# A hybrid state-space and gated-recurrence block: another model for the instruction scheduler, and other steps for scan, GELU, carry and output weight loads

## The chip, the cores and the metric

The kernel runs on one core of one Trainium2 chip. The metric is the device time of one execution in microseconds; the time before is 1541.35 us, the median of 3 runs (1541.31 to 1543.61).

## What is computed

One decoder block over 2048 rows of width 1024, in float32. The input is normalised, projected once to 5632 columns, and split into two branches; their outputs are projected, gated, merged, projected again and added to the input.

```python
xn = rms_norm(h, norm_w)
u_a, z_a, q_b, f_b, i_b, og_b, z_b, g_a, g_b = jnp.split(xn @ w_in, SPLIT_POINTS, axis=-1)
# branch A: 32 groups, each a complex diagonal state of 64, by an associative scan over the rows
y = C h + d * u;  y = gelu(y);  y = y * sigmoid(y @ w_glu + b_glu);  y_a = y * silu(z_a)
# branch B: 4 heads, gated recurrence in chunks, output gate, norm per head
state = exp(last) * state + k exp(last - cum) v;  y_b = rms_norm(o * sigmoid(og)) * silu(z_b)
merged = sigmoid(g_a) * (y_a @ w_proj_a) + sigmoid(g_b) * (y_b @ w_proj_b)
out = rms_norm(h + merged @ w_out, final_norm_w)
```

## The kernel before, in words

The rows are worked in two halves of 1024 (a = 0 and 1). Every float32 operand of a large matmul is split into a rounded part and a rest (`split`, lines 118 to 120: one ACTIVATE on ScalarE for the first, one subtraction on VectorE for the second), and each product is three matmuls (high by high, high by rest, rest by high).

The stages follow each other. First some projections are done plainly (`plain`). Then comes a Strassen stage for the first half (`strassen(0, s0)`, 18 slices of 256 columns) and one for the second half (`strassen(1, s1)`, 22 slices). A slice is seven products of 12 matmuls of 512 columns (lines 458 to 460); its results gather in PSUM banks of a pool of four, are copied out on ScalarE (`snap`, L464) or added on VectorE (`total`, L467), and go to an `evac` function. Weights are split at their first use, stored to DRAM as `wc` and loaded from there in the second half (L375, three products ahead, in a ring of five buffers). Behind them stand, for each half, two GLU passes (`glu`), the merge of the branches (`merge`) and the output projection (`out_proj`), in which `narrow` does one half of the columns, one tile of 128 rows after the other.

Other work is laid beside these dense stages by hand. `timed(dense, n, events)` runs the dense generator for n steps and calls, before each step, the events that are due at it; `steps(ev, g, at)` puts the parts of a generator, divided by its `yield`s, at the steps of a list. So are laid out: the recurrence of branch B (`hgrn_block`, levels 0 to 8 and two more parts), the tables of the scan (`ssm_build`), the scan in 16 batches of four groups (`ssm_batch`: loads of WU and VM, for a = 0 the cosine and sine tables from E, matmuls into psg, the scan on VectorE, matmuls into psy, a store to y_d), `gelu` (a load of yy, four ACTIVATEs that reorder it, Square, two operations on VectorE, Sigmoid, a multiplication, a store to ya_d), `glu_prep` (reloads of that, and splits) and `out_w` (a load of the output weights, and splits).

TensorE's order is that of the program text (`tc.manual_schedule` for this engine). The order of ScalarE, VectorE, GpSimd and SyncE is made at build time by the framework's scheduler: it plays the program on a model of the chip and hands each engine, of the instructions that the model holds ready, the one that stands earliest in the text. On the chip each engine then runs its list in order. Nearly all loads and most stores are issued by SyncE (SP); some stores by ScalarE. Buffers come from pools with tags: `wr` (3 buffers, `wr4`), `wo` (5), `y` (2, `y4`), `s` (5), `e` (2), `r` (56).

## Time and profile before

| | before |
|---|---|
| median of 3 runs | 1541.35 us |
| the profiled execution | 1540.05 us |
| its span, first to last instruction | 1538.3 us |
| PE (matmul) busy | 1467.0 us, 95%, 7360 instructions |
| PEld (weight load) busy | 1207.3 us, 78% |
| DVE (VectorE) busy | 1100.8 us, 72%, 2409 instructions |
| ACT (ScalarE) busy | 637.6 us, 41%, 1391 instructions |
| DMA | 354.53 MB, mean 230 GB/s |

A matmul's busy time overlaps with that of its neighbours, so a busy PE is read together with the time from one start to the next. The granted clock is given as a share of 2.4 GHz. In a timeline row, the bracket at the end is the engine's idle time before the instruction and what ended it; the count after x is how many like instructions are merged in the row.

### The profile page before, as it was taken

Reading aid. Unit: us, or ns where it says so; the run is one execution under the profiler, and the core shown is the slowest. Engines: PE = TensorE matmul, PEld = TensorE weight load, DVE = VectorE, ACT = ScalarE, POOL = GpSimd, SP = SyncE. Lnnn points to the kernel's source line nnn. Section 1 sums busy time; section 2 is a strip of 40 time slices with the busy share of each in tenths; the row PEclk is TensorE's granted clock in tenths of the full one; section 3 lists DMA queues with packets and bytes.
Section 4 is the critical chain, followed back from the end, with each engine's and each line's share of the span. In section 5 each row is a group of like instructions: output and inputs, shape, how many; then the busy total and the mean of one; then the engine's idle time right before and its main releaser. Section 6 shows DMA issues by size and latency. Waiting matters only on the chain.

```text
span 1538.3 us, 21386 instructions
## 1 busy us (share of the span) xinstructions
PE 1467.0 (95%) x7360; PEld 1207.3 (78%) x7360; DVE 1100.8 (72%) x2409; ACT 637.6 (41%) x1391; POOL 3.6 (0%) x24
## 2 busy tenths in 40 slices
PE   7997999999999999999989999999989899899997
PEld 5776788788888777878878887788878688688886
DVE  5798688678678659956665887776649877765445
ACT  7456454454454634323323455333353332532222
POOL 0000000000000000000000000000000000000000
PEclk9998999999999999999999999999999999999999
DMA  9539778977977883786668559677977854854602
GB/s 336 175 115 305 284 278 295 316 255 269 331 264 286 285 271 119 186 245 197 231 201 313 174 163 294 217 259 264 327 236 234 266 184 137 274 171 131 212 14 103
DMA packets 192060, 354.53 MB, mean 230 GB/s; under 512 B 65680, under 2 KB 74896, under 8 KB 191952
## 3 DMA queue, kind: packets, MB, share of 16 engines
q1 hardware_dynamic: 163792, 328.00, 63.6%
q10 hardware_dynamic: 28160, 25.17, 4.8%
q8 instruction: 58, 0.95, 0.3%
q14 instruction: 50, 0.41, 0.1%
HBM read 214.17 MB, written 138.94 MB: 230 GB/s over the span
## 4 chain that ended last, share of the span: by engine, by line
PE 68%; DVE 15%; DMA 10%; ACT 3%; issue 3%; SPq 0%; ACTq 0%; DVEq 0%
PE pd L458 14%; PE pd L460 13%; PE pd L459 13%; PE pf L1284 3%; PE pf L1285 3%; PE pf L1286 3%; PE pp L1112 2%; PE pp L1111 2%; PE pp L1110 2%; PE sc L979 2%; DMA y_d<-T 1%; DVE w L120 1%; DMA xb<-in_xt_dram 1%; DMA xq<-xo_d 1%; PE pd L355 1%
## 5 line engine op out<-in xcount | busy, mean ns | idle before, releaser
L119 ACT ACTIVATE w<-rw 128x512 fp32r<-128x512 f32 x110 | 68.7, 628 | 112.7 <-PE pd L460 67.9
L1284 PE MATMUL pf<-ho,mh 128*128 128x512 f32 x256 | 101.2, 395 | 5.2 <-ACT mh L119 5.2
L1286 PE MATMUL pf<-ho,ml 128*128 128x512 f32 x256 | 100.6, 393 | 0.5 <-DVE ml L120 0.5
L1285 PE MATMUL pf<-lo,mh 128*128 128x512 f32 x256 | 100.3, 392 | 0.0
L464 ACT ACTIVATE u<-pd 128x512 f32<-128x512 f32 x80 | 47.5, 594 | 106.0 <-PE pd L460 103.3
L120 DVE TENSOR_TENSOR w<-rw,w 128x512 fp32r<-128x512 f32 x110 | 75.3, 685 | 16.9 <-ACT w L119 16.6
L467 DVE TENSOR_TENSOR u<-u,pd 128x512 f32<-128x512 f32 x80 | 54.8, 685 | 33.5 <-PE pd L460 22.8
L355 PE MATMUL pd<-xh,hw 128*128 128x512 f32 x128 | 52.4, 409 | 9.0 <-ACT hw L119 6.7
L1284 PEld LDWEIGHTS pf<-ho,mh 128*128 128x128 f32 x256 | 48.6, 190 | 15.4 <-ACT mh L119 5.5
L1286 PEld LDWEIGHTS pf<-ho,ml 128*128 128x128 f32 x256 | 48.4, 189 | 11.6 <-DVE ml L120 1.6
L1285 PEld LDWEIGHTS pf<-lo,mh 128*128 128x128 f32 x256 | 48.6, 190 | 9.9
L119 ACT ACTIVATE mh<-sgl 128x512 fp32r<-128x512 f32 x32 | 20.0, 629 | 86.7 <-DVE sgl L1227 86.3
L356 PE MATMUL pd<-xl,hw 128*128 128x512 f32 x128 | 51.2, 400 | 0.0
L357 PE MATMUL pd<-xh,lw 128*128 128x512 f32 x128 | 50.9, 397 | 0.0
L980 DVE COPY_PREDICATED s_buf<-masks,sc 128x256 f32<-128x256 uint8 x64 | 32.5, 508 | 25.0 <-PE sc L979 25.0
L1110 PE MATMUL pp<-yh,hpa 128*128 128x512 f32 x128 | 50.2, 392 | 0.0
L1112 PE MATMUL pp<-yh,lpa 128*128 128x512 f32 x128 | 49.9, 390 | 0.2 <-DVE lpa L120 0.2
L1111 PE MATMUL pp<-yl,hpa 128*128 128x512 f32 x128 | 50.0, 390 | 0.0
L1226 DVE TENSOR_TENSOR sgl<-sgl,pp 128x512 f32<-128x512 f32 x48 | 32.7, 683 | 23.0 <-PE pp L1112 22.9
L1016 DVE TENSOR_TENSOR Q<-Q,t 128x256 f32<-128x256 f32 x96 | 40.5, 422 | 10.0 <-PE sc L991 9.9
L974 ACT ACTIVATE KX<-K 128x128 f32<-128x128 f32 x128 | 32.6, 304 | 35.6 <-DVE K L1017 26.3
L979 PEld LDWEIGHTS sc<-Q,KX 128*128 128x128 f32 x256 | 38.0, 189 | 8.9 <-issue 1.8
(915 smaller groups left out, 4431.6 us busy)
## 6 DMA issues: line engine op xcount, KB each, us to landing
wc<-w SPq DMA_DIRECT2D x126, 512.0 KB, 3.4
w<-wc SPq DMA_DIRECT2D x126, 512.0 KB, 4.6
rw<-in_wi_dram SPq DMA_DIRECT2D x44, 512.0 KB, 4.6
sgl<-sg_d SPq DMA_DIRECT2D x48, 256.0 KB, 3.2
sg_d<-u ACTq DMA_DIRECT2D x32, 256.0 KB, 3.5
ro<-in_wo_dram SPq DMA_DIRECT2D x16, 512.0 KB, 5.1
hh<-in_xn_dram SPq DMA_DIRECT2D x32, 256.0 KB, 5.1
out_dram<-hh SPq DMA_DIRECT2D x32, 256.0 KB, 2.4
```

Of the source, the lines that this page charges most:

```text
L119: S.activation(hi, raw, AF.Copy)
L120: V.tensor_tensor(lo, raw, hi.bitcast(F32), op=ALU.subtract)
L458: mm(o, w[:, 0, k], xh, start=(first and k == 0), stop=False, skip_group_check=True)
L459: mm(o, w[:, 0, k], xl, start=False, stop=False, skip_group_check=True)
L460: mm(o, w[:, 1, k], xh, start=False, stop=(k == 3), skip_group_check=True)
L979: mm(ps[:, :, c, :], ch(kx, c), qp, start=True, stop=True)
L1110: mm(ps, hi[:, k, fs], yh, start=(k == 0), stop=False)
L1111: mm(ps, hi[:, k, fs], yl, start=False, stop=False)
L1112: mm(ps, lo[:, k, fs], yh, start=False, stop=(k == last))
L1284: mm(o, mh[:, ts_], hi, start=(kk == 0), stop=False)
L1285: mm(o, mh[:, ts_], lo, start=False, stop=False)
L1286: mm(o, ml[:, ts_], hi, start=False, stop=(kk == 7))
```

## The change

The tile context gets `schedule_with_timeline_sim=True`: the scheduler plays the program on another, the timeline model, before it orders the engines other than TensorE. Beside it the steps and the text order of several pieces are changed:

- `ssm_batch`: the loads are no longer all at the first part. For a = 0, E is loaded first, then after two parts W and U, then V and M; the stores of the cosine and sine tables stand behind the first use of psg. For a = 1 the tables, W and U come first, V and M a part later. The first part of a batch is at step -7 (was -5) for a = 0; in the second pass a batch is laid at 4 + 7i (was 6 + 7i).
- `gelu` is divided by `yield`s into five parts, which are put at steps of their own: the reordering copies three steps behind the load, the rest in the steps after.
- `hgrn_block`: the load of the carried state moves from the start of the block to level 6.
- `out_w` gets a `yield` between load and split, and its parts are put at other steps; `narrow` looks the split weights up when it uses them, not before it begins.
- `glu_prep(1, 0)` is one step later; the raw weights of the second half's first QF slice come from the pool `wr`, not `y`.

```diff
@@ -379,7 +379,7 @@
             wc_d[sl] = [dram.tile([128, 1024], F32, name=f"wc{sl}_{p}") for p in range(7)]
 
         def get(kh):
-            raw = (y4 if a and sl != SL_VO else wr4)(f"rw{n}_{kh}").rearrange("p (k n) -> p k n", k=4)
+            raw = (y4 if a and sl < SL_QF else wr4)(f"rw{n}_{kh}").rearrange("p (k n) -> p k n", k=4)
             nc.sync.dma_start(raw, wi[sl, kh])
             return raw[:, :, 0:128], raw[:, :, 128:256]
 
@@ -751,39 +751,39 @@
         sh = [128, 4, 8, 16]
         t4 = lambda n: sp.tile(sh, F32, name=f"{n}{a}{b}", tag="s")
         flat = lambda t: t.rearrange("p g a b -> p g (a b)")
-        WU = wu_pool(f"WU{a}{b}").rearrange("p (i g n) -> p i g n", i=2, g=4)
-        VM = vm_pool(f"VM{a}{b}").rearrange("p (i g n) -> p i g n", i=2, g=4)
-        Wt, U = WU[:, 0], WU[:, 1]
-        Vt, Mt = VM[:, 0], VM[:, 1]
-        nc.sync.dma_start(Wt, w_d[:, gs, :])
-        nc.sync.dma_start(U, u_d[a][b // 2][:, :, g0 : g0 + 4, :].rearrange("s p g c -> (s p) g c"))
-        nc.sync.dma_start(Vt, v_d[:, gs, :])
-        nc.sync.dma_start(Mt, m_d[:, gs, :])
-        CC, SS = t4("CC"), t4("SS")
         csv = lambda i: cs_d[b][:, i].rearrange("p (g a b) -> p g a b", g=4, a=8)
-        T = t4("T")
         if a == 0:
             E = sp.tile([128, 4, 48], F32, name=f"E{b}", tag="e", bufs=2)
             nc.sync.dma_start(E[:, :, 0:32], el_d[:, gs, :])
             nc.sync.dma_start(E[:, :, 32:48], eh_d[:, gs, :])
+            yield
+        CC, SS = t4("CC"), t4("SS")
+        T = t4("T")
+        if a == 0:
             lr_ = E[:, :, 0:16].unsqueeze(2).to_broadcast(sh)
             li_ = E[:, :, 16:32].unsqueeze(2).to_broadcast(sh)
             hr_ = E[:, :, 32:40].unsqueeze(3).to_broadcast(sh)
             hi_ = E[:, :, 40:48].unsqueeze(3).to_broadcast(sh)
-            yield
             V.tensor_tensor(CC, lr_, hr_, op=ALU.mult)
             V.tensor_tensor(T, li_, hi_, op=ALU.mult)
             yield
             V.tensor_tensor(CC, CC, T, op=ALU.subtract)
             V.tensor_tensor(SS, lr_, hi_, op=ALU.mult)
-            yield
-            V.tensor_tensor(T, li_, hr_, op=ALU.mult)
-            V.tensor_tensor(SS, SS, T, op=ALU.add)
-            nc.sync.dma_start(csv(0), CC)
-            nc.sync.dma_start(csv(1), SS)
         else:
             nc.sync.dma_start(CC, csv(0))
             nc.sync.dma_start(SS, csv(1))
+        WU = wu_pool(f"WU{a}{b}").rearrange("p (i g n) -> p i g n", i=2, g=4)
+        Wt, U = WU[:, 0], WU[:, 1]
+        nc.sync.dma_start(Wt, w_d[:, gs, :])
+        nc.sync.dma_start(U, u_d[a][b // 2][:, :, g0 : g0 + 4, :].rearrange("s p g c -> (s p) g c"))
+        yield
+        if a == 0:
+            V.tensor_tensor(T, li_, hr_, op=ALU.mult)
+            V.tensor_tensor(SS, SS, T, op=ALU.add)
+        VM = vm_pool(f"VM{a}{b}").rearrange("p (i g n) -> p i g n", i=2, g=4)
+        Vt, Mt = VM[:, 0], VM[:, 1]
+        nc.sync.dma_start(Vt, v_d[:, gs, :])
+        nc.sync.dma_start(Mt, m_d[:, gs, :])
         C2, S2 = flat(CC), flat(SS)
         yield
         ps = pss.tile([128, 4, 128], F32, name=f"psg{a}{b}", tag="pss")
@@ -793,6 +793,9 @@
         V.tensor_tensor(t1, ps, C2, op=ALU.mult)
         V.tensor_tensor(t2[0:64], ps[64:128], S2[64:128], op=ALU.mult)
         V.tensor_tensor(t2[64:128], ps[0:64], S2[0:64], op=ALU.mult)
+        if a == 0:
+            nc.sync.dma_start(csv(0), CC)
+            nc.sync.dma_start(csv(1), SS)
         yield
         V.tensor_tensor(t1, t1, t2, op=ALU.add)
         hv = h0[:, gs]
@@ -835,18 +838,22 @@
     GE = 2.0 * math.sqrt(2.0 / math.pi)
 
     def gelu(a, i):
-        ya = wr4(f"ya{a}{i}")
         yy = y4(f"yy{a}{i}").rearrange("p (t c) -> p t c", t=8)
         nc.sync.dma_start(yy, y_d[a][i].rearrange("t p g c -> (p g) t c"))
+        yield
+        ya = wr4(f"ya{a}{i}")
         for i4 in range(4):
             c0 = i4 * 256
             dst = ya[:, c0 : c0 + 256] if i4 % 2 == 0 else ya[:, c0 + 255 : (c0 - 1 if c0 else None) : -1]
             S.activation(dst.rearrange("p (c t) -> p t c", t=8), yy[:, :, i4 * 32 : i4 * 32 + 32], AF.Copy)
         q = yy.rearrange("p t c -> p (t c)")
         S.activation(q, ya, AF.Square)
+        yield
         V.tensor_scalar(q, q, 0.044715, 1.0, op0=ALU.mult, op1=ALU.add)
         V.tensor_tensor(q, q, ya, op=ALU.mult)
+        yield
         S.activation(q, q, AF.Sigmoid, scale=GE)
+        yield
         V.tensor_tensor(ya, ya, q, op=ALU.mult)
         nc.sync.dma_start(ft_d["ya", a, i], ya)
 
@@ -937,9 +944,6 @@
         K = h2("K" + n, "K")
         V.tensor_scalar(K, F, -1.0, 1.0, op0=ALU.mult, op1=ALU.add)
         Sb = s_buf[b]
-        if a == 1 and b == 0:
-            cin = e2("ci" + n)[:, 0:128]
-            nc.sync.dma_start(cin, carry_d[h])
         KX = h2("KX" + n, "x")
         V.tensor_tensor(KX, K, Q, op=ALU.mult)
         kh = hp.tile([128, 512], F32R, name="kh" + n, tag="st")
@@ -983,6 +987,9 @@
                     ps.rearrange("p a c (j m) -> p a (c j) m", m=m),
                 )
             elif lv <= 7:
+                if lv == 6 and a == 1 and b == 0:
+                    cin = e2("ci" + n)[:, 0:128]
+                    nc.sync.dma_start(cin, carry_d[h])
                 ps = psc.tile([128, 4, 128], F32, name=f"sc{n}_{lv}", tag="psc")
                 for hf in range(2):
                     for r in range(0, 128, 2 * m):
@@ -1252,6 +1259,7 @@
                 continue
             raw = wr4(f"ro{a}{nh}{kp}").rearrange("p (k n) -> p k n", k=2)
             nc.sync.dma_start(raw, wo[nh, kp])
+            yield
             res = ow[a, nh, kp] = []
             for k in range(2):
                 hi = pool.tile([128, 512], F32R, name=f"ho{a}{nh}{kp}{k}", tag="r")
@@ -1339,14 +1347,14 @@
                     if tt % 2:
                         yield
 
-        def narrow(nh, w):
+        def narrow(nh):
             for tt in range(8):
                 x_load(nh, tt)
                 if nh == 1:
                     V.tensor_scalar(fss[:, tt : tt + 1], fss[:, tt : tt + 1], -0.5 / D, -0.5 * EPS, op0=ALU.mult, op1=ALU.add)
                 o = psd.tile([128, 512], F32, name=f"pf{a}{nh}{tt}", tag="psd")
                 for kp in range(4):
-                    products(nh, kp, tt, o, w[kp])
+                    products(nh, kp, tt, o, ow[a, nh, kp])
                     if kp == 1:
                         yield
                 add_x(nh, tt, o)
@@ -1355,10 +1363,10 @@
                 yield
 
         if a == 0:
-            yield from narrow(0, [ow[a, 0, kp] for kp in range(4)])
+            yield from narrow(0)
         else:
             yield from wide(0, {})
-        yield from narrow(1, [ow[a, 1, kp] for kp in range(4)])
+        yield from narrow(1)
 
     def run(*gens):
         for g in gens:
@@ -1505,10 +1513,11 @@
         batches = [ssm_batch(0, b, wr4, wr4) for b in range(8)] + [ssm_batch(1, b, wr4, wr4) for b in range(2)]
         for i, g in enumerate(batches):
             t = 62 + 9 * i
-            for d in ((-5, -4, -3, -2) if i < 8 else (-3,)) + (0, 1, 2, 3, 6):
+            for d in ((-7, -4, -3, -2) if i < 8 else (-4, -2)) + (0, 1, 2, 3, 6):
                 ev.append((t + d, lambda g=g: step(g)))
             if i % 2:
-                ev.append(((101, 106, 118, 136, 151)[i // 2], lambda i=i: gelu(i // 8, i // 2 % 4)))
+                t = (98, 105, 116, 134, 150)[i // 2]
+                steps(ev, gelu(i // 8, i // 2 % 4), [t, t + 3, t + 4, t + 5, t + 6])
         steps(ev, glu_prep(0, 0), [146, 147, 148, 149])
         steps(ev, glu_w(), [150, 151, 152, 153])
         timed(d1, 154, ev)
@@ -1518,14 +1527,15 @@
         steps(ev, glu_prep(0, 1), [0, 1, 2, 3])
         for i in range(6):
             g = ssm_batch(1, i + 2, y4, wr4 if i < 2 else wo4f, (psm, "psm"))
-            t = 6 + i * 7
-            for d in (-3, 0, 1, 2, 3, 6):
+            t = 4 + i * 7
+            for d in (-4, -2, 0, 1, 2, 3, 6):
                 ev.append((t + d, lambda g=g: step(g)))
             if i % 2:
-                ev.append((t + 7, lambda i=i: gelu(1, i // 2 + 1)))
-        steps(ev, out_w(0, 0, range(4), rp), [14 + s for s in range(8)])
-        steps(ev, out_w(0, 1, range(4), rp), [28 + s for s in range(8)])
-        steps(ev, glu_prep(1, 0), [51, 52, 53, 54])
+                steps(ev, gelu(1, i // 2 + 1), [t + 7, t + 10, t + 11, t + 11, t + 12])
+        for kp in range(4):
+            steps(ev, out_w(0, 0, (kp,), rp), [12 + 2 * kp, 15 + 2 * kp, 16 + 2 * kp])
+            steps(ev, out_w(0, 1, (kp,), rp), ([24, 27, 28], [26, 29, 30], [36, 40, 40], [37, 41, 41])[kp])
+        steps(ev, glu_prep(1, 0), [52, 53, 54, 55])
 
         def lazy(f):
             yield from f()
@@ -1542,7 +1552,8 @@
         for i in range(8):
             steps(ev, yb_load(1, i // 2, i % 2), [i // 2 + 2, i // 2 + 4])
         steps(ev, out_w(1, 0, (0,), None), [21])
-        steps(ev, out_w(1, 1, (2, 3), rp), [26, 27, 28, 29])
+        for kp in (2, 3):
+            steps(ev, out_w(1, 1, (kp,), rp), [19 + 2 * kp, 22 + 2 * kp, 23 + 2 * kp])
         steps(ev, out_w(1, 1, (0, 1), None), [37, 38])
         mg1 = merge(1)
         ev += [(4, lambda: step(mg1)), (6, lambda: step(mg1))]
@@ -1636,7 +1647,7 @@
         args.append(nc.dram_tensor(f"in_{name}_dram", a.shape, mybir.dt.from_np(a.dtype), kind="ExternalInput").ap())
     o = nc.dram_tensor("out_0_dram", (L, D), F32, kind="ExternalOutput")
     args.append(o.ap())
-    with tile.TileContext(nc) as tc:
+    with tile.TileContext(nc, schedule_with_timeline_sim=True) as tc:
         hybrid_block(tc, *args)
     r = run_bass_kernel_spmd(nc, [arrays], core_ids=[0])
     return np.ascontiguousarray(_order(np.asarray(r.results[0]["out_0_dram"]).reshape(L, D))).reshape(1, L, D)
```

## Rows read from the trace of the kernel before

**Rows 1.** The page's line of busy time by engine, and the span with the mean granted clock.
```profile
PE 1467.0 (95%) x7360; PEld 1207.3 (78%) x7360; DVE 1100.8 (72%) x2409; ACT 637.6 (41%) x1391; POOL 3.6 (0%) x24
...
core 0: 1538.3 us, clock 0.984
```
**Rows 2.** The view of windows. Columns: the stretch in us, its length, then busy us (and instructions) of PE, PEld, DVE, ACT and POOL, the mean granted clock, the mean busy share of the 16 DMA engines, and GB/s.
```profile
120.00:160.00 40.00, 33.40 (x151) 27.62 (x150) 34.08 (x104) 23.36 (x55) 0.00 (x0) 0.89 0.93 321
...
240.00:280.00 40.00, 40.00 (x197) 33.63 (x196) 34.70 (x78) 18.67 (x41) 0.00 (x0) 1.00 0.82 297
...
500.00:560.00 60.00, 54.90 (x283) 43.58 (x282) 40.78 (x81) 36.31 (x85) 0.00 (x0) 0.97 0.81 274
...
760.00:800.00 40.00, 37.40 (x219) 31.01 (x218) 27.75 (x63) 11.70 (x28) 0.00 (x0) 1.00 0.67 205
800.00:840.00 40.00, 38.06 (x233) 31.26 (x232) 23.72 (x50) 9.79 (x24) 0.10 (x1) 0.96 0.90 315
...
1120.00:1145.00 25.00, 19.36 (x81) 15.63 (x80) 8.47 (x12) 9.70 (x16) 0.00 (x0) 0.86 0.68 227
...
1160.00:1200.00 40.00, 40.00 (x198) 33.66 (x197) 38.49 (x70) 11.55 (x19) 0.00 (x0) 1.00 0.72 241
1200.00:1240.00 40.00, 33.19 (x142) 26.57 (x141) 32.92 (x60) 15.57 (x28) 0.00 (x0) 0.87 0.84 280
...
1320.00:1360.00 40.00, 32.74 (x127) 25.67 (x126) 30.57 (x65) 20.94 (x38) 0.00 (x0) 0.91 0.73 246
```
**Rows 3.** The timeline of PE in a quiet stretch and behind a long wait.
```profile
269.75 0.39 PE L459 MATMUL pd<-X014l,w 128*128 128x512 f32 x1
...
271.34 0.39 PE L460 MATMUL pd<-X034h,w 128*128 128x512 f32 x1
...
1134.61 0.79 PE L458 MATMUL pd<-X105h,w 128*128 128x512 f32 x1 [5.64 <-ACT u L464]
...
1138.62 0.55 PE L458 MATMUL pd<-X135h,w 128*128 128x512 f32 x1
```
**Rows 4.** The timeline of ACT at the end of the second Strassen stage.
```profile
1130.90 2.09 ACT L844 ACTIVATE ya<-yy 128x256 f32<-128x256 f32 x4 [6.73 <-DMA yy<-y_d]
...
1133.98 0.58 ACT L464 ACTIVATE u<-pd 128x512 f32<-128x512 f32 x1
```
**Rows 5.** The timelines of ACT, DVE and PE where the merge of the first half ends and its output projection begins.
```profile
1211.94 2.14 ACT L844 ACTIVATE ya<-yy 128x256 f32<-128x256 f32 x4 [3.57 <-DMA yy<-y_d]
...
1215.21 0.69 DVE L847 TENSOR_SCALAR yy<-yy 128x1024 f32<-128x1024 f32 x1 [3.41 <-ACT yy L846]
...
1223.83 0.66 DVE L1227 TENSOR_TENSOR sgl<-sgl,sgl 128x512 f32<-128x512 f32 x1
...
1225.21 0.79 PE L1284 MATMUL pf<-ho,mh 128*128 128x512 f32 x1 [5.22 <-ACT mh L119]
```
**Rows 6.** The timelines of ACT, SP and PE around the first GLU pass of the second half.
```profile
1300.02 0.58 ACT L831 ACTIVATE T<-psy 128x512 f32<-128x512 f32 x1
...
1316.09 0.33 SPq L851 DMA_DIRECT2D ya_d<-ya  x1
...
1322.70 0.52 SPq L1178 DMA_DIRECT2D gy<-ya_d  x1
...
1328.27 0.63 ACT L119 ACTIVATE gh<-gy 128x512 fp32r<-128x512 f32 x1 [2.93 <-DMA gy<-ya_d]
...
1328.95 0.50 PE L1110 MATMUL pg<-gh,gwh 128*128 128x512 f32 x1 [3.87 <-ACT gh L119]
...
1345.09 0.50 PE L1110 MATMUL pg<-gh,gwh 128*128 128x512 f32 x1 [2.83 <-ACT gh L119]
```
**Rows 7.** The timeline of SP, which issues the DMAs, where the first scan batch is loaded.
```profile
775.10 0.38 SPq L375 DMA_DIRECT2D w<-wc  x1
780.06 0.32 SPq L863 DMA_DIRECT2D zb_d<-ezb  x1
...
786.56 0.33 SPq L375 DMA_DIRECT2D w<-wc  x1
...
800.56 6.27 SPq L375 DMA_DIRECT2D w<-wc  x5
```
**Rows 8.** The view of waits over the whole span, of SP's queue and of the engines. Columns: who waited, for whom, us in total, times, the longest.
```profile
SPq L391 <- DVE w L120: 173.3, 87, 8.3
...
SPq L782 <- DVE CC L777: 21.8, 6, 12.3
...
ACT ya L844 <- DMA yy<-y_d: 22.5, 6, 6.7
...
PE pd L458 <- ACT u L464: 13.4, 4, 6.6
...
PE pd L458 <- DMA w<-wc: 4.5, 2, 2.6
```
**Rows 9.** The view of DMA issues: the load of the carried state, its count, size and median us to landing.
```profile
ci<-carry_d SPq DMA_DIRECT2D x4, 64.0 KB, 3.6
```
**Rows 10.** The timeline of ACT early in the first Strassen stage.
```profile
129.23 1.06 ACT L191 ACTIVATE xr<-xr 128x1024 f32<-128x1024 f32 x1 [2.61 <-DMA xr<-in_xn_dram]
...
130.69 0.57 ACT L464 ACTIVATE u<-pd 128x512 f32<-128x512 f32 x1
```

## The prediction

> **What bounds the kernel now.** I read the page's busy times first, then the table of windows for stretches where TensorE (PE) falls short, then the timelines of the other engines around each shortfall. PE is busy 1467.0 of 1538.3 us and the mean granted clock is 0.984 [rows 1]. In a quiet stretch it is busy all 40 of 40 us [rows 2], and its 512-column matmuls start every 0.227 us: seven intervals in 1.59 us [rows 3]. So PE is the bound, and the work that it does is not changed: the change neither adds nor removes a matmul. What can be won is what PE loses: 1538.3 - 1467.0 = 71.3 us of idle time, and about (1 - 0.984) x 1538.3 = 24.6 us in clock, the two overlapping a little. The reader should see in rows 2 that this is lost in a few places. Idle plus clock deficit is about 7 + 4 us at 120:160, 5 + 2 at 500:560, 5 + 2 at 760:840, 5.6 + 3.5 at 1120:1145, 6.8 + 5.2 at 1200:1240 and 7.3 + 3.6 at 1320:1360. A long wait costs twice: behind the one at 1134.61 the next matmuls start every 0.44 us (nine intervals in 4.01 us, the 1.2 GHz level), 2.0 us more than nine of 0.227 [rows 3].
>
> **The change part by part.** PE's order is written by hand; each step of a dense stage is mostly 12 such matmuls, 12 x 0.227 = 2.7 us. ACT, DVE and SP run in the order that the scheduler's model of the chip gave them at build time, so an instruction that the model held ready and the chip does not holds up everything behind it.
>
> *A. GELU in steps, end of the second Strassen stage.* ACT stood 6.73 us in front of GELU's copies (L844), waiting for the load of yy; the PSUM snapshot (L464) behind them came at 1133.98, and PE, which needed that bank, waited 5.64 us [rows 3, 4]. The loss is 5.64 + 2.0 = 7.6 us. The change states the load at step 150 and the copies at 153, three steps or 8.2 us apart, so the snapshots of the steps between stand ahead of them. No instruction is added. What is late next is the first GLU products just behind, which need their own loads. I take 7 us won, bounds 0 and 7.6.
>
> *B. GELU and scan batches beside the first merge.* ACT waited 3.57 us for yy, DVE therefore 3.41 us; DVE's queue then reached the sum of the gates (L1227) only at 1223.83, and PE waited 5.22 us for what is made from it [rows 5]. Idle is 6.8 us and the clock deficit 5.2 in that window [rows 2], 11.5 us when the overlap is taken off. But DVE is itself busy 38.49 of 40 us just before [rows 2]. Starting each scan batch two steps earlier (4 + 7i for 6 + 7i) puts the whole third batch ahead of the output projection, not half of it: two sevenths of a batch more on DVE, about 2 us. So the 3.41 us that DVE stood come back, and some 2 us of them are spent again; with the clock that would follow a shorter wait I take 4.5 us won, bounds 0 and 11.5.
>
> *C. Last GELU into the second GLU.* The last scan output leaves PSUM at 1300.02; GELU's result is stored at 1316.09; SP issues the reload only at 1322.70, behind output stores; the split ends the wait, and PE idles 3.87 us, then 2.83 us at the next GLU [rows 6]. With the matmuls stated two steps earlier this chain starts 5.5 us sooner, while glu_prep(1, 0) is stated one step (2.7 us) later; that step only orders, since the data comes last. The first wait goes, with 1.7 us of clock (half of the 3.6 deficit). The second is a chain of loads behind the first, and PE will come to it 4 us sooner too: I leave it as it is. 3.87 + 1.7 = 5.6, plus the short waits beside it: 6 us won, bounds 2 and 10.5.
>
> *D. Loads and stores of the scan batches on SP.* From 775.10 SP stood still until a store at 780.06, then issued six scan loads, and the next weight load came at 786.56; the m_d and cos/sin stores ended before the load of 800.56 [rows 7]. PE waited twice for such weights, 4.5 us in all [rows 8]. The change spreads the six loads of a batch over three steps, and puts the cos/sin stores behind the first matmuls; SP had stood 21.8 us for them, 12.3 us at once [rows 8]. Their 16 issues only move. I take 2.5 us won of the 6 us lost in 760:840, bounds -2 and 6. The DMA engines' share in 800:840 is 0.90 [rows 2]. The Trainium skill (DMA: Bandwidth & Descriptors, Issuing engines are not separate DMA queues) says that transfers run on the same 16 engines whoever starts them and that issuing elsewhere saves only issue time; if that also holds of issuing in another order, D is 0 and the time below 2.5 us longer.
>
> *E. Edits with one answer.* The other four GELUs: of ACT's 22.5 us of waits for yy some 12 lie there [rows 8], and no long PE wait follows: 0, bounds 0 and 3. The carry load goes from the block's start to level 6; it lands in 3.6 us [rows 9] and has three levels of two blocks, six steps or 16 us, before it is used: 0, and 4 x 3.6 us if that cover were gone. The first weights of the second pass load into another pool, away from the reloads of X: 0, between -3 and 3 (ACT's wait of 3.57 us in rows 5 is the size of one such collision). out_w(1, 1) two to seven steps sooner: 0, for PE loses nothing in 240:280 [rows 2] either, with the same lead of loads. out_w(0, 1): its last two parts are split at steps 40 and 41, when the second half of the projection already runs and their buffers have only just come free; it costs at most one step, 2.7 us, at least 0; I take 1 us lost.
>
> *F. The model.* It reorders ACT, DVE and SP everywhere, also where no step was moved, and no row shows its order. For it: at 129.23 ACT waited 2.61 us for a row of x with a snapshot behind that PE needed [rows 10], and 120:160 and 500:560 lose 18 us together [rows 2]; a model that dates transfers better would win up to that. Against: the stretches where PE loses nothing now can only lose; the bound is a wait like A's, 7.6 us, three or four times. I take 0, bounds -18 and 28: nothing in the trace leans either way.
>
> Sum: 7 + 4.5 + 6 + 2.5 - 1 + 0 = 19 us. The profiled execution took 1540.05 us (span 1538.3 and 1.75 around it), 1.3 us less than the median of 1541.35: 1540.05 - 19 + 1.3 = 1522 us.
>
> **The rivals.**
> *Slower: the new order puts stores ahead of weight loads.* Both Strassen stages hold 40 slices of seven products. SP stood 173.3 us, 87 times, in stores of split weights that wait for DVE [rows 8]; a weight load that the new order puts behind such a store comes late, and PE's ring is only three products ahead. For it: the one long SP wait above did reach PE. Against: PE waited for such loads 4.5 us in all [rows 8]. It cancels the gain from 19/40 = 0.5 us a slice; at 0.8 us it gives 1541 - 19 + 32 = 1554 us.
> *No difference: the waits move on.* In B, DVE's 38.49 of 40 us stay the bound and give 0; A's wait becomes one for the GLU's inputs right behind; D is bound by transfers; C keeps 4 us; the projection costs 2.7. 1541 - 4 + 2.7 = 1540 us. For it: the DVE figure and the 0.90 share. Against: A and C are single instructions standing in front of others with the engine idle.
> *The flag does not change the order.* Then only the stated steps act, through priorities, with the old model's dates: half of A and D, all of C and B: 3.5 + 4.5 + 6 + 1 - 1 = 14, or 1527 us.
>
> **How the numbers follow.** The forecast 0.65, the slower rival 0.18, no difference 0.12, the flag idle 0.05. Faster by over 0.2% (3 us, about what a measurement of this kernel can tell from no change) is 0.65 + 0.05 = 0.70; within it 0.12; slower 0.18. The range: 1522 with F's gain and the larger ends of B and C would be near 1495, of which I leave out the last 2 us; upward it takes in the two faster cases, no difference, and the slower rival up to 0.75 us a slice, 1552. What is left out is about 0.1 below and 0.1 above.
>
> **What would show it.** A: in the window around the second stage's end no ACT wait for yy ahead of a snapshot, and PE busy over 24 of 25 us. B: DVE without the 3.4 us hole, PE's wait for the merged operand under 4 us. C: PE's first wait for gh gone, the second still near 3 us. D: no PE wait on a weight load in the scan batches. F: the stretches 120:160 and 500:560 within some us of now. The prediction is wrong if PE's idle time in the first 500 us, where no step was moved, changes by over 10 us either way, or if the waits of A to C come back at new places in front of other loads.

## The result, and the profile after

The changed kernel takes 1562.01 us (median of 4 runs, 1559.56 to 1566.78) where the kernel before took 1541.33 us beside it (1540.19 to 1543.61). The ratio is 1.0136, with a 95% interval of 1.0107 to 1.0165: slower by 21 us. The forecast was 1522 us, faster, with a range that ended at 1552; it was wrong in its sign and missed its range. The profiled execution took 1566.78 us, 4.8 us over the median, so the places below add up to some 5 us more than the medians do.

First the page after, its line of busy time by engine and the mean granted clock; they answer to [rows 1].

```profile
PE 1472.5 (94%) x7360; PEld 1210.5 (77%) x7360; DVE 1099.6 (70%) x2409; ACT 637.0 (41%) x1391; POOL 4.2 (0%) x24
...
core 0: 1565.0 us, clock 0.976
```

The work is the same, 7360 matmuls. PE's idle time grew from 71.3 to 92.5 us and the clock fell from 0.984 to 0.976. Next the view of windows after, with the columns of [rows 2]; the second half of the program runs some 25 us later than before, so its rows are to be read that much shifted.

```profile
120.00:160.00 40.00, 25.12 (x110) 20.37 (x109) 22.72 (x71) 18.94 (x40) 0.00 (x0) 0.77 0.78 293
240.00:280.00 40.00, 35.90 (x162) 29.50 (x161) 31.68 (x69) 17.72 (x40) 0.00 (x0) 0.91 0.75 283
500.00:560.00 60.00, 55.53 (x314) 45.15 (x313) 44.11 (x92) 37.39 (x91) 0.00 (x0) 0.98 0.84 295
760.00:800.00 40.00, 40.00 (x238) 32.64 (x237) 27.12 (x57) 13.90 (x32) 0.00 (x0) 1.00 0.76 248
...
1120.00:1165.00 45.00, 32.94 (x143) 26.51 (x142) 22.23 (x49) 18.61 (x35) 0.00 (x0) 0.89 0.67 211
1200.00:1240.00 40.00, 38.43 (x193) 32.07 (x192) 35.99 (x65) 13.71 (x25) 0.00 (x0) 1.00 0.82 266
1240.00:1280.00 40.00, 34.68 (x166) 28.81 (x165) 31.49 (x61) 12.92 (x24) 0.00 (x0) 0.96 0.79 276
```

At 120:160, where no step was moved, PE's idle time went from 6.6 to 14.9 us and the clock from 0.89 to 0.77. 240:280, where PE lost nothing, now has 4.1 us idle and a clock of 0.91. 760:800 lost 2.6 us and now loses nothing. Windows cannot be subtracted once the programs have drifted apart. So I took the start of every dense matmul (their order is the same in all kernels) and subtracted its start in the trace of before. This lag is worked out from two traces, in us, at some points of the kernel before:

| start in before | 25 | 100 | 125 | 160 | 310 | 560 | 815 | 1100 | 1125 | 1150 | 1185 | 1245 | 1300 | 1340 | 1529 |
|---|---|---|---|---|---|---|---|---|---|---|---|---|---|---|---|
| after | -0.4 | 4.1 | 1.1 | 9.9 | 15.1 | 16.3 | 7.9 | 18.3 | 23.4 | 24.0 | 30.3 | 28.0 | 28.0 | 24.0 | 26.7 |
| e1, steps alone | 0.3 | 0.2 | 0.3 | 0.2 | -0.3 | 0.6 | 2.6 | 4.8 | 6.4 | 7.5 | 7.9 | 13.6 | 13.6 | 7.4 | 11.6 |
| e2, model alone | -0.3 | 3.9 | 1.0 | 9.6 | 13.1 | 13.9 | 6.4 | 13.3 | 19.3 | 19.7 | 21.7 | 19.9 | 19.9 | 17.3 | 17.8 |
| e7, shift alone | 0.1 | 0.0 | 0.0 | -0.7 | 1.1 | 0.3 | -0.3 | -0.5 | 0.1 | 0.2 | 0.3 | 5.2 | 5.2 | -1.1 | 3.8 |
| e9, best | 0.2 | 0.2 | 1.6 | -6.7 | -5.7 | -6.3 | -6.0 | -5.8 | -4.2 | -11.2 | -8.1 | -13.4 | -12.7 | -13.1 | -12.3 |

The reader should see three stretches in the row of after: 16 us lost by 560, some 8 us of them won back by 815, and 15 us lost between 815 and 1125. All step edits are stated behind 560; one load that they move, the first of the carried state, SP issues near 200 us in every order, and e1's lag stays within 0.6 us up to there. Each row is of one execution: at its end it can differ from the difference of medians by up to 6 us.

The largest single loss is at 140 us. This is PE's row of before behind the same snapshot (ACT's is in [rows 10]), then the timeline of ACT after, and the PE rows behind it.

```profile
131.32 0.80 PE L458 MATMUL pd<-X004h,w 128*128 128x512 f32 x1 [6.60 <-ACT u L464]
```

```profile
127.36 1.06 ACT L191 ACTIVATE xr<-xr 128x1024 f32<-128x1024 f32 x1 [4.00 <-DMA xr<-in_xn_dram]
...
137.64 1.06 ACT L191 ACTIVATE xr<-xr 128x1024 f32<-128x1024 f32 x1 [4.70 <-DMA xr<-in_xn_dram]
...
138.69 1.04 ACT L191 ACTIVATE xr<-xr 128x1024 f32<-128x1024 f32 x1
...
139.73 0.57 ACT L464 ACTIVATE u<-pd 128x512 f32<-128x512 f32 x1
...
140.36 0.79 PE L458 MATMUL pd<-X004h,w 128*128 128x512 f32 x1 [14.54 <-ACT u L464]
140.95 0.63 PE L459 MATMUL pd<-X004l,w 128*128 128x512 f32 x1
...
143.08 0.63 PE L458 MATMUL pd<-X024h,w 128*128 128x512 f32 x1
```

ACT stood 4.00 and 4.70 us for rows of x, and the snapshot that PE needed lay behind all these Squares. PE waited 14.54 us where it had waited 6.60; behind it the matmuls start every 0.426 us (five intervals in 2.13 us), the 1.2 GHz level. That level did not last:

```profile
140.00:145.00 5.00, 4.64 (x11) 3.67 (x12) 1.85 (x10) 1.99 (x4) 0.00 (x0) 0.50 0.63 217
145.00:150.00 5.00, 4.66 (x22) 3.75 (x22) 1.38 (x7) 2.77 (x6) 0.00 (x0) 1.00 0.60 209
```

Most of the low clock in 120:160 was granted while PE stood, so it must not be added to the idle time.

A smaller place shows the queue of SP. The view of one source line, L699: 28 small stores of zeros into m_d, first before, then after, with the shortest, median and longest issue in ns and their first and last start; then SP, DVE and PE after.

```profile
L699 SPq DMA_DIRECT2D m_d<-zt x28: 423/445/1954, 198.6 to 432.8; - x28
```

```profile
L699 SPq DMA_DIRECT2D m_d<-zt x28: 303/436/912, 208.7 to 238.0; - x28
...
231.83 0.42 SPq L383 DMA_DIRECT2D rw<-in_wi_dram  x1
...
237.97 0.69 DVE L400 TENSOR_TENSOR s<-rw,rw 128x512 f32<-128x512 f32 x1 [4.24 <-DMA rw<-in_wi_dram]
...
245.93 1.12 PE L918 MATMUL pt<-ident,u 128*128 128x128 f32 x4 [4.10 <-DVE u L467]
```

The stores were spread over 234 us and now stand within 29 us. The raw weights that DVE is about to add are issued only at 231.83, DVE stands 4.24 us for them, and PE, which needs a sum behind that on DVE, waits 4.10 us where it did not wait before.

The start shows the same: the rows of x for the first statistics are issued on SP at 13.95 before and at 20.52 after, behind more loads of xp and rw, masks and a bias.

```profile
13.95 5.06 SPq L186 DMA_DIRECT2D xr<-in_xn_dram  x8
```

```profile
17.12 0.33 SPq L508 DMA_DIRECT2D mf<-in_msk_dram  x1
...
19.15 0.33 SPq L510 DMA_DIRECT2D bg_t<-in_bg_dram  x1
...
20.52 5.12 SPq L186 DMA_DIRECT2D xr<-in_xn_dram  x8
...
35.54 1.86 PE L205 MATMUL psn<-dg,ones 128*128 128x512 f32 x2 [3.97 <-DVE small L169]
```

### The profile page after: what moved, and what is told of

It is laid out like the page before. It is cut to its first block, busy times and chain, and to the rows that moved or that the text cites. A ratio compares the mean times of both kernels' runs of the same rounds, so it can differ in the third digit from the quotient of the medians.

```text
span 1565.0 us, 21433 instructions
## 1 busy us (share of the span) xinstructions
PE 1472.5 (94%) x7360; PEld 1210.5 (77%) x7360; DVE 1099.6 (70%) x2409; ACT 637.0 (41%) x1391; POOL 4.2 (0%) x24
## 4 chain that ended last, share of the span: by engine, by line
PE 62%; DVE 9%; DMA 9%; issue 2%; ACT 2%; SPq 1%; ACTq 0%; DVEq 0%
PE pd L458 11%; PE pd L460 11%; PE pd L459 11%; PE pf L1293 4%; PE pf L1292 4%; PE pf L1294 4%; PE pp L1119 2%; PE pp L1118 2%; PE pp L1117 2%; DMA rw<-in_wi_dram 1%; DMA rpa<-in_wp_dram 1%; PE sc L983 1%; DMA y_d<-T 1%; DMA xq<-xo_d 1%; PE pb L1118 1%
## 5 line engine op out<-in xcount | busy, mean ns | idle before, releaser
L1300 ACT ACTIVATE pf<-hh 128x512 f32<-128x512 f32 x32 | 19.2, 600 | 63.1 <-DVE hh L1298 63.1
```

## The experiments

Intervals are 95%. Times of different experiments are compared by their ratios to the kernel before on the same chip, turned into us with 1541.

**The two halves of the change.** e1 has every step edit and not the model; e2 is the kernel before with the model.

```diff
 e1: after, but
-    with tile.TileContext(nc, schedule_with_timeline_sim=True) as tc:
+    with tile.TileContext(nc) as tc:
 e2: before, but
-    with tile.TileContext(nc) as tc:
+    with tile.TileContext(nc, schedule_with_timeline_sim=True) as tc:
```

> All the moved steps, the scheduler's old model. Theory M (the new model's order costs, the steps win): the kernel is faster than before, 1541 less the 10 to 18 us that scan batches, merge and last GLU win, 1523 to 1531 us, and PE's idle time in the first 500 us is as before. Theory S (the steps cost, the model's order is neutral): as slow as the changed kernel, 1555 to 1565 us. Theory X (each fits the other only): slower than before by some other amount, with waits at places that neither of the two profiles has.

> The new model, no step moved. Theory M: slower than the changed kernel, since it pays the same 16 us in the first 560 us and lacks the steps' gain: 1565 to 1580 us, with the long wait near 140 us in place. Theory S: as before, 1538 to 1546 us. Theory X: over 1580 us.

Measured: e1 1547.18 us, ratio 1.0054 (1.0035 to 1.0073), 8 us slower than before. e2 1559.91 us, ratio 1.0141 (1.0122 to 1.0159), 22 us slower. The model alone costs as much as the whole change, and most of it at the same places (the table's third row, and the wait of e2 below). The steps alone are not a gain either; beside the model they are worth about nothing (1.0136 against 1.0141). No theory held for both: of M the model's cost came true and the steps' gain did not, and of X the wait at a new place (in e1, 4.86 us at 802.60) but not the time of e2.

```profile
139.77 0.79 PE L458 MATMUL pd<-X004h,w 128*128 128x512 f32 x1 [14.03 <-ACT u L464]
```

**The wait at 140 us.** e3 is the changed kernel with the row statistics of the second half stated in parts: each load three or so steps ahead of its Square.

```diff
-        ev += [(2, lambda: stats(0)), (8, lambda: stats(1)), (13, lambda: bcast(0)), (18, lambda: bcast(1))]
+        ev += [(13, lambda: bcast(0)), (18, lambda: bcast(1))]
+        steps(ev, stats(0), [2, 5, 6, 8, 9])
+        steps(ev, stats(1), [9, 12, 13, 15, 16])
```

> The changed kernel, in which the row statistics of the second half (loads of x, Square, sums) are stated in parts: each Square three or more steps behind its load. If ACT, held by a Square whose load has not landed, is what makes PE wait 14.5 us near 140 us, that wait falls under 4 us and the kernel is 8 to 14 us faster than the changed one, 1548 to 1554 us. If PE waits there for something else (the split of weights on DVE, which also waits for a load of weights), the wait stays over 10 us and the time within 3 us of 1562.

Measured: 1551.44 us, ratio 1.0087 (1.0069 to 1.0105), 7.5 us faster than the changed kernel by the ratios. The 14.5 us went; half of it came back as a new wait of 8.2 us for a snapshot at 156 us, behind the next Squares. So the wait hung on the Squares, as the first theory had it, and the gain fell just short of its 8 to 14 us.

e8 does the same to the kernel before.

> Kernel before with one edit that the change doesn't have: the row statistics of the second half are stated in parts, each Square some three steps behind the load of its row. The wait for a snapshot near 131 us (6.6 us idle and a stretch at half clock) should go. Theory 'gain stays': 5 to 9 us faster than before, 1529 to 1534 us. Rival 'given back' (in the changed kernel 8.5 of the 16.5 us won were lost again 30 us later): 0 to 3 us faster, 1535 to 1539 us.

Measured: 1531.94 us, ratio 0.9943 (0.9927 to 0.9959), 9 us faster than before, and the gain stays, as the theory of that name had it (lag -9.1 at 160, -10.0 at the end). The window row of e8 that answers to the first of [rows 2]:

```profile
120.00:160.00 40.00, 40.00 (x206) 32.96 (x205) 35.26 (x99) 25.84 (x58) 0.00 (x0) 0.98 0.94 344
```

PE is busy all 40 of 40 us there, where before it was 33.40. The same edit wins 7.5 us under one model and 9 under the other, so 22 us remain between e3 (all of the change) and e8 (none of it): the 140-us wait is a place of the cost, not the whole.

**The wait at the end of the second Strassen stage (A).** e4 is the changed kernel with the GELU of the second half's first quarter stated beside the GLU and the merge.

```diff
+        steps(ev, gelu(1, 0), [3, 7, 8, 8, 9])
```

> The changed kernel with the first GELU of the second half stated beside the GLU and merge (steps 3 to 9 of the next stage), not at the end of the Strassen stage. If its copies in front of the snapshot are what holds PE for 7.0 us near 1159 us, that wait goes and 7 to 11 us are won, 1551 to 1555 us, as far as DVE, busy in the merge, bears three more operations; if it does not, the wait before the output projection grows and the time is within 3 us of 1562.

Measured: 1561.49 us, ratio 1.0146 (1.0117 to 1.0174): nothing won. PE's wait at 1159 fell from 6.97 to 2.73 us, and from 1125 to 1150 the lag falls by 3.3 us where after it rises by 0.6. The merge lost it again: from 1150 to 1245 the lag rises by 7.7 us, after by 4.0, with DVE busy 39.32 of 40 us at 1200:1240. Of the theory's 7 to 11 us the wait came true and the gain did not.

**Which steps cost.** All three have the model of before. e5 keeps only the edits beside the second Strassen stage; e6 has all but the shift of the second pass's batches; e7 has that shift alone.

```diff
 e5: second pass as before: t = 6 + i * 7, all loads of a batch at -3, GELU in one part, out_w and glu_prep(1, 0) at their old steps
 e6: all steps, but
-            t = 4 + i * 7
+            t = 6 + i * 7
 e7: before, but
-            t = 6 + i * 7
+            t = 4 + i * 7
```

> Kernel before with the model that it has, and of the step edits only those beside the second Strassen stage (scan batches of the first half, GELU in steps there, carry load, pool of the raw weights); the second pass stands at the steps of before. Theory 'two places': what all steps cost, 9 us, is about 7 us at one place beside the second Strassen stage (a split weight loaded behind a batch's W and U) and about 2 us net in the second pass, so this kernel is 5 to 8 us slower than before, 1544 to 1547 us. Rival 'all in the second pass': within 2 us of before, 1537 to 1541 us.

> All step edits, old model, but the scan batches of the second pass stay at steps 6 + 7i instead of 4 + 7i. Theory 'shift': starting the batches two steps earlier puts more of a batch on VectorE in front of the rest of the merge's operand, so without it TensorE's wait of 6.2 us for that rest goes, before's wait of 5.2 us for the other operand comes back, and the gain at the second GLU goes: 1543 to 1547 us. Rival 'loads': it is the later loads of W and U within a batch that cost, so the waits stay, the gain at the second GLU goes and the time rises over that of all steps: 1550 to 1555 us.

> Kernel before with one edit: the scan batches of the second pass at 4 + 7i instead of 6 + 7i. Theory 'shift': the merge loses 7 to 9 us net and the second GLU gains 6, so 1 to 3 us slower than before, 1539 to 1542 us. Rival 'loads': the merge's loss belongs to the other edits, the gain at the second GLU stays and the wait of 5.2 us in the merge goes with it: 6 to 15 us faster, 1524 to 1533 us.

Measured: e5 1539.05 us, ratio 0.9993 (0.9977 to 1.001), no difference; e6 1547.1 us, 1.0039 (1.0021 to 1.0056); e7 1544.96 us, 1.0031 (1.0019 to 1.0044). My 'two places' fell: the steps beside the second Strassen stage cost nothing in sum, and all 8 us lie in the second pass. Both the shift (5 us) and the other edits there (about 6 us without it) bring a wait for the same split; whether their costs add up the intervals do not tell. e6's time lies at the edge of the range of 'shift', but by luck: the wait of 5.2 us did not come back (5.5 us for the split lpa stand in its place), and the gain at the second GLU stayed (lag from 12.9 to 8.0 between 1300 and 1340). e7 is slower by more than the 1 to 3 us of 'shift', since the second GLU kept 1.4 us of the 6 that I expected. In e7 it shows on DVE, ahead of the PE row:

```profile
1209.07 0.68 DVE L120 TENSOR_TENSOR lpa<-rpa,hpa 128x512 fp32r<-128x512 f32 x1
...
1213.04 1.20 DVE L848 TENSOR_TENSOR yy<-yy,ya 128x1024 f32<-128x1024 f32 x1
...
1216.13 1.20 DVE L850 TENSOR_TENSOR ya<-ya,yy 128x1024 f32<-128x1024 f32 x1
...
1218.83 0.68 DVE L120 TENSOR_TENSOR lpa<-rpa,hpa 128x512 fp32r<-128x512 f32 x1
...
1219.57 0.80 PE L1112 MATMUL pp<-yh,lpa 128*128 128x512 f32 x1 [7.65 <-DVE lpa L120]
```

Between one split of the merge's weights and the next stand 9 us of scan, GELU and other splits, with DVE idle for 1.1 of them.

**Where GELU stands.** e9 is the kernel before with e8's edit, and the first two GELUs of the second half behind the merge, beside the output projection, their input in the pool `wo`. e10 and e11 move scan batches on top of it, e12 adds the model.

```diff
 e9
+        steps(ev, gelu(1, 0), [20, 24, 25])
+                    steps(ev, gelu(1, 1), [22, 27, 28])
 e10: e9, and
-            t = 6 + i * 7
+            t = (6, 13, 20, 26, 32, 38)[i]
 e11: e9, and
-            t = 6 + i * 7
+            t = 4 + i * 7
 e12: e9 with schedule_with_timeline_sim=True
```

> Kernel before with the row statistics in parts (as in e8), and the GELUs of the second half's first and second quarter moved behind the merge, beside the output projection (loads at steps 20 and 22, the rest at 24 to 28; their input in the pool wo). Theory 'placed, not modelled': the wait near 1125 us (5.0 us and 2 us of clock) and the one at the merged operand near 1216 us (5.1 us and part of 10 us of half clock) both hang on a GELU that stands on ScalarE or VectorE where TensorE needs them next; with it away they go, 10 to 15 us beyond e8: 1517 to 1523 us. Rival 'the waits move on': the GLU's inputs or VectorE's load take their place and nothing is won over e8: 1530 to 1534 us.

> e9, and the last three scan batches of the second pass 1, 2 and 3 steps earlier (26, 32, 38 for 27, 34, 41), all behind the merge. Theory: the wait at the second GLU near 1320 us (4 us and half clock) shrinks without a loss in the merge, 4 to 6 us beyond e9. Rival: the second wait there, 2.6 us, grows by as much, and at most 2 us are won over e9.

> e9, and the scan batches at 4 + 7i instead of 6 + 7i (the edit that cost 5 us alone in e7). Theory 'VectorE in front of the merge': in e7 GELU's 3 us of VectorE time and the scan stood between two splits of the merge's weights, so with GELU away the wait of 7.6 us for that split falls under 4 us, and the shift costs at most 2 us over e9. Rival: the scan alone fills VectorE there, the wait stays over 6 us, and the shift costs 5 us again.

> e9 with the timeline model. Theory 'a few waits': the model's cost of 22 us in e2 hung on the same instructions that e8 and e9 move (the wait of 14 us at 140 us, the GELU waits), so here it falls to 6 to 12 us over e9. Rival 'spread': the model's order puts late transfers and long chains of small operations ahead everywhere, so it costs 18 to 24 us here too.

Measured: e9 1529.39 us, ratio 0.9905 (0.9876 to 0.9935), 14.6 us faster than before; no kernel of the study is faster. It wins 6 us on e8 by the ratios, which come from two chips and whose intervals just overlap; the 10 to 15 were too much. PE's wait at the merged operand fell from 5.22 to 0.63 us and the one at the end of the Strassen stage from 5.64 to 0.69; the waits at the second GLU stayed (3.44 and 3.80 us):

```profile
1120.00:1145.00 25.00, 23.64 (x102) 18.61 (x100) 11.22 (x17) 11.31 (x19) 0.00 (x0) 1.00 0.63 213
1200.00:1240.00 40.00, 37.33 (x164) 30.76 (x164) 36.06 (x69) 17.82 (x31) 0.00 (x0) 0.91 0.87 290
```

against 19.36 of 25 us and 33.19 of 40 us in [rows 2]. e10 1531.96 us, ratio 0.9916 (0.9883 to 0.9949): nothing won on e9; PE waits 3.6 us for a load of WU instead. e11 1535.32 us, ratio 0.9954 (0.9935 to 0.9973), 7.5 us slower than e9: the wait for the split halved (4.06 us), but the shift costs as much as in e7 or more (in the traces, 10 us of lag on e9 between 1150 and 1245). Why is not shown: its profiled execution was 9.6 us over its median, and of the 5 us of DVE work between the two splits the scan is under half. e12 1553.39 us, ratio 1.0064 (1.0046 to 1.0083), 24.5 us slower than e9: the number of 'spread'. The model costs the same on a kernel in which the old order's worst waits were taken away. But its trace shows no even spread. Of the 25 us of lag on e9, 12.7 are there at 160 us, where the wait for the snapshot behind the Squares is back (8.14 us at 158.31, the one that e3 has too); 4.8 us more are lost by 310, 9.1 won between 560 and 815, and 17.4 lost between 815 and 1150.

**One queue.** What of the model's order costs was still open. e13 is e12, e14 the changed kernel and e15 e9, each with the 28 stores of zeros issued by GpSimd, so that they leave SP's queue.

```diff
-                nc.sync.dma_start(
+                nc.gpsimd.dma_start(
                     m_d[s * 16 : s * 16 + 16, g0 : g0 + 8, 0 : 16 * s],
```

> e12 (the timeline model) with the 28 zero stores of m_d issued by GpSimd instead of SyncE. Theory 'SyncE's order': the raw weights near 229 us are then issued some us earlier, VectorE's stand of 6.0 us and TensorE's wait of 5.8 us for what is behind it go, with 1 to 2 us of clock: 5 to 8 us faster than e12, 1545 to 1549 us where e12 had 1553. Rival 'the transfer itself is late or VectorE is full': within 2 us of e12.

> The changed kernel with the 28 zero stores of m_d issued by GpSimd. Theory: VectorE's stand of 4.2 us near 238 us and TensorE's wait of 4.1 us near 246 us go, 4 to 6 us faster than the changed kernel, a ratio of 1.0095 to 1.011 to the kernel before. Rival: within 2 us of it, 1.0125 to 1.015.

> Control: e9 (the model of before) with the same 28 stores issued by GpSimd. There they were spread over SyncE's queue and nothing waited for them: theory and rival both expect the time of e9 within 2 us, a ratio near 0.9905. A gain of 4 us or more here would say that the stores cost on any order, and would take the third place away from the model.

Measured: e13 1550.63 us, ratio 1.005 (1.0032 to 1.0067); e14 1561.31 us, 1.0118 (1.0091 to 1.0146); e15 1529.01 us, 0.9911 (0.9881 to 0.9941). At the place itself the theory holds. In e12 the raw weights were issued at 228.59, DVE stood 5.98 us for them and PE 5.84 us; in e13 they were issued at 223.60, DVE had no wait, and PE's was 0.45 us. First e12, then e13:

```profile
228.59 0.43 SPq L383 DMA_DIRECT2D rw<-in_wi_dram  x1
...
235.50 0.70 DVE L400 TENSOR_TENSOR s<-rw,rw 128x512 f32<-128x512 f32 x1 [5.98 <-DMA rw<-in_wi_dram]
...
243.45 1.11 PE L913 MATMUL pt<-ident,u 128*128 128x128 f32 x4 [5.84 <-DVE u L467]
```

```profile
223.60 0.44 SPq L383 DMA_DIRECT2D rw<-in_wi_dram  x1
...
230.41 0.69 DVE L400 TENSOR_TENSOR s<-rw,rw 128x512 f32<-128x512 f32 x1
...
239.03 0.66 PE L913 MATMUL pt<-ident,u 128*128 128x128 f32 x4 [0.45 <-DVE u L467]
```

By the lag PE won 6.7 us on e12 there, and 5.9 us in e14 on the changed kernel. By the ratios only 2 to 3 us of it are left at the end, and the intervals overlap, so both times lie between theory and rival, short of the 5 to 8 and 4 to 6 us expected. The stores now run at 2.9 to 23.6 us, and PE's wait for the first row sums near 36 us grew from 4.7 to 6.3 us (e12 to e13). Where the rest went is not shown: e13's trace gives it back in pieces behind 560, but its profiled execution was the slowest of the ten. In e15 the edit does nothing, as it should where the stores were spread out.

## Why the prediction was wrong

The forecast was 19 us won and 21 were lost: a miss of 40 us. Two steps failed, of nearly the same size. F was taken at 0 and costs 22 us. The sum of A to E was taken at 19 us won; it is worth about nothing beside the model (e2 against the whole change) and loses 8 us without it (e1).

**F, the model: the larger step that failed.** I took 0 and wrote that nothing in the trace leans either way. It is +22 us on the kernel before (e2) and +24 on e9 (e12). The upper bound of 28 held it; the value taken did not. The chance was wrong as well: with a term that reaches from -18 to 28 and nothing to say for 0, a forecast of faster at 0.70 rested on steps whose sum, 19 us, was no larger than that term's spread. The words on it were right: the stretches where PE loses nothing could only lose, and 240:280 did. Its test was also right: PE's idle time in the first 500 us rose from 24.2 to 35.8 us. (A slip in the range decides nothing: 1522 less 18, 7 and 4.5 us is 1492.5, not near 1495.)

What the runs show of it, at two places: the model's order puts instructions that are fed by a transfer ahead of ones that PE is about to need, and bunches small stores on SP ahead of loads. For the stores at L699, e13 to e15 show it by taking them off the queue in both orders. For the Squares at 140 us, the traces show it, and e3 that the wait hangs on them. That the model dates transfers too early everywhere is only argued: the losses between 815 and 1125 (13 us net in e2, one of them a wait of 5.09 us for ACT at 1131 after) were not taken apart by a run.

**A.** 7 us taken, none won: PE waited 6.97 us there after, 5.64 before.

```profile
1144.82 0.37 ACTq L835 DMA_DIRECT2D y_d<-T  x1
...
1151.09 1.15 ACT L119 ACTIVATE gwh<-rg 128x512 fp32r<-128x512 f32 x2 [3.56 <-DMA rg<-in_wg_dram]
...
1152.17 0.37 SPq L842 DMA_DIRECT2D yy<-y_d  x1
...
1156.25 2.09 ACT L848 ACTIVATE ya<-yy 128x256 f32<-128x256 f32 x4 [4.01 <-DMA yy<-y_d]
...
1158.67 0.58 ACT L464 ACTIVATE u<-pd 128x512 f32<-128x512 f32 x1
...
1159.30 0.79 PE L458 MATMUL pd<-X105h,w 128*128 128x512 f32 x1 [6.97 <-ACT u L464]
```

The store of the scan's output is issued at 1144.82 and the load that reads it only at 1152.17, when that store has landed (7.3 us). I counted the three steps from the statement of the load, not from the store behind which it must wait: on SP such loads stood 32.3 us for y_d stores, 7 times, 8.9 us at the longest. Before, the same view has 32.4 us, 6 times, 11.0 at the longest: the row was there to be read. The size was right: with GELU elsewhere, in e9, the lag falls by 7.0 us from 1125 to 1150.

**B.** 4.5 us taken; the shift alone loses 4.9 us between 1185 and 1245 (e7), and the steps together 5.7 (e1). I saw that DVE was full (38.49 of 40 us), priced the two sevenths of a batch at 2 us, and charged them only against the operand behind the merge. They fell on the splits of the merge's own weights, a wait that takes the place of the one removed. With the old model the lower bound of 0 was therefore wrong: a move into a full engine can lose. In the changed kernel the lag falls by 2.3 us between 1185 and 1245, but it falls by 1.8 in e2 too, where no step was moved: beside the model B is worth about nothing there. The changed kernel loses 6.3 us just ahead, between 1150 and 1185 (e2: 2.0); no run takes that apart.

**C.** 6 us taken, 1.3 to 2 won. The first wait went as said (lag -4.0 after, -6.3 in e7, from 1300 to 1340), and the second, which I left as it was, gave most of it back: 2.7 us after, 4.9 in e7, with DVE's splits of gh late. The model without the steps has as much there (-2.6 and 0.5 in e2).

```profile
1364.03 0.51 PE L1117 MATMUL pg<-gh,gwh 128*128 128x512 f32 x1 [2.15 <-ACT gh L119]
1365.43 0.51 PE L1118 MATMUL pg<-gl,gwh 128*128 128x512 f32 x1 [0.89 <-DVE gl L120]
...
1369.04 0.80 PE L1118 MATMUL pg<-gl,gwh 128*128 128x512 f32 x1 [1.00 <-DVE gl L120]
```

**D.** PE's two waits for weights are gone after, as forecast, but the model does that without D: 780 to 815 wins 6.7 us after and 6.7 in e2, where the batches' loads are not spread. With the steps and the old model the first wait goes, worth 2.8 us of lag in e1, and a longer one of 4.86 us for such a load follows (at 802.60). Of all stretches, the model's order wins most in this one. The Trainium skill (DMA: Bandwidth & Descriptors, Issuing engines are not separate DMA queues) says that issuing from another engine saves only issue time, usually small beside the transfer. The traces agree on the size: a store of zeros took 0.45 us to issue on SP and 3.4 us to land (medians, kernel before). But 28 such issues ahead of a load that PE's chain needs are not small: with them gone from SP, e13 won 6.7 us at that place. How much of it is issue time no run tells, since the transfers left that stretch as well.

**E.** The edits beside the second Strassen stage together with A and D come out at 0 (e5), where A and D were taken at 9.5 us won; E's part of it was not taken apart. Of out_w I took 1 us lost, and of the later loads of WU in the second pass nothing; in e6 the edits there bring waits of 1.65 us for a split and 2.94 us for a load of WU in the projection, beside those in the merge.

**The rivals.** 'Slower' had the right sign and another mechanism: SP's order does matter, but not through stores of split weights on every slice (SP stood for those 154.8 us after, less than the 173.3 of [rows 8]). 'The waits move on' is what happened to C and, with the old model, to B, and 'the flag does not change the order' is excluded by e2.

## What to carry to other kernels

A switch that reorders every queue is a term of its own: price it by what the present order already hides, and run it alone first. Move a piece of work out of the stretch where another one needs its engine, not by a step or two within it: e8 won 9 us by parting the Squares from the snapshots, and e9 some 6 more by moving two GELUs, where the whole list of finer steps won nothing. Count a load's lead from the store that it must wait for, not from the step at which it is stated.

## What was not expected of the hardware

The same 28 stores took 0.45 us of issue each on SP and landed after 3.4 us (medians, kernel before); issued by GpSimd they took 0.53 us and 5.0 us (e13), though in another stretch of the kernel, so the difference is not of the queue alone.

A wait twice as long cost no more clock. Behind the 6.60 us of before PE ran at the lower level from 131.32 to 135.43, and behind the 14.54 us after from 140.36 to 144.97: 4.1 and 4.6 us at 0.426 us a matmul in place of 0.227, by estimate some 2 us lost each time. The mean granted clock of 120:160, 0.89 and 0.77, suggests far more, because the clock was low during the wait as well (0.50 in 130:140 after).
